# Latent attention on one core: a head's scores alternate with the last head's transposes, and a pair's products with v are issued two key tiles at a time, one step later

## The chip, the cores and the metric

One core of a Trainium2 chip. The metric is the device time of one execution in microseconds (us), lower is better. TensorE (PE in the profile, its weight loads PEld), VectorE (DVE), ScalarE (ACT) and GpSimd (POOL) each work through their own list of instructions in order and wait for each other by semaphores; SyncE (SP) issues the transfers.

## The reference

The program is a long chain: one transformer block with dilated attention, spatial gating and experts, then a retention and state-space layer with a gated feed-forward layer, then latent attention with a second feed-forward layer, all in float32. The change lies in the latent attention alone. There 512 latent tokens attend to 768 keys (256 context and 512 latent tokens), in 16 heads:

```
kv = rms_norm(ckv)                        # 768 x 256 compressed channels
k  = concat(kv @ w_uk[h], rope(k_pe))     # 64 + 32 channels, per head
q  = rms_norm(cq) @ w_uq                  # 512 x (16 x 96)
v  = kv @ w_uv                            # 768 x (16 x 64)
p  = softmax(q[h] @ k[h].T / sqrt(96))    # 512 x 768, per head
o[h] = p @ v[h]                           # 512 x 64
h1 = h + gate * (concat(o) @ w_mo)
```

## The kernel before

Everything is unrolled. The Python code records the instructions in program order; a list scheduler of the framework then fixes each engine's order once, when the program is built, with the place in the code as its priority. So the order within an engine is near that of the code, but a piece whose inputs come later may be cut up and moved behind others.

**The tiles.** Queries are cut into 4 tiles of 128 tokens (`qt`), keys into 6 tiles of 128 (`kt`), heads into 8 pairs. For each head `queries` transposes its 96 query channels (tile `qtb`, split into a high and a low part `qT`); `keys` makes a pair's keys in two pieces of 512 and 256 columns (tile `kb`, split into `kT`). `scores` makes, for each `qt`, a 128 x 768 tile `sc` by six matmuls (three split passes on 512 and on 256 columns), takes its row maximum (DVE, L1795), the exponential with its row sum (ACT, L1796), the reciprocal (DVE, L1797) and scales the probabilities `Pm` (L1798; POOL for `qt` 0, DVE for the other three). `spread(h, kt)` transposes one key tile of all four `Pm` tiles into a bank `ptb` (four transposes) and copies it out as `PTm`: DVE for `kt` 0 and 3, ACT for the other four.

**The products.** `ob` of a pair is one bank of 128 rows: the first head of the pair (`a_` = 0) writes rows 0 to 63 through the columns 0 to 63 of TensorE's array, the second (`a_` = 1) rows 64 to 127 through the columns 64 to 127. Each of the pair's 12 products (2 heads x 6 key tiles) is one float32 matmul of 512 columns, for which the trace has two records.

**The order.** A loop takes the heads one by one. Step `h` issues the keys of the next pair (every other step) and the queries of head `h` + 1, the four score tiles of head `h`, and then works on head `h` - 1: if that is the first of a pair, its six `spread`; if it is the second, `values`, in which each `spread` is followed at once by the two products of its key tile:

```
for kt in range(6):
    spread(2 * hp + 1, kt)
    for a_ in range(2):
        K.mm(ob[64 * a_:...], v[...], pts[h, kt // 2][:, kt % 2, :], kt == 0, kt == 5, ...)
```

**The buffers.** Of the eight PSUM banks `sc` has two tiles of two banks, `ptb` and `qtb` share two, `kb` and `ob` have one each. `Pm` tiles lie in the ring `wr` of 6, which also takes raw weights, so the loads of the next stage's weights `w_mo` wait until the last `Pm` tiles are read. The other stages of the program are the same before and after.

Of the kernel before, what the change touches and what calls it, by code (L numbers as in the profile page):

```python
# [7 lines left out]
F32 = mybir.dt.float32  # L8
# [21 lines left out]
# ---------------------------------------------------------------- host layout  # L30
def tile_a(w, kc=2, nb=512):
    """[K, N] -> [N/nb, K/(128 kc), 128, kc, nb], each chunk contiguous per partition."""
    k, n = w.shape
    return np.ascontiguousarray(w.reshape(k // (P * kc), kc, P, n // nb, nb).transpose(3, 0, 2, 1, 4))


def tile_b(w):
    """[K, M] -> [M/128, 128, K/128, 128]."""
    k, m = w.shape
    return np.ascontiguousarray(w.reshape(k // P, P, m // P, P).transpose(2, 1, 0, 3))  # L40


def cols(v):
    """vector [n*128] -> [128, n]."""
# [3 lines left out]
def shape_consts():  # L48
# [7 lines left out]
    c["amask"] = m[3 * P:]                                             # depends on i - j alone  # L56
    c["rinv"] = np.tile((np.float32(500000.0) ** (-np.arange(0, 16, 2, dtype=np.float32) / np.float32(16)))[None], (P, 1)).astype(np.float32)
    c["utri"] = (i[:, None] <= i[None, :]).astype(np.float32)      # [s, t]: s <= t
# [3 lines left out]
    d2 = (i[None, :] - i[:, None]).astype(np.float32)                 # [j, i]: i - j  # L62
# [14 lines left out]
def axial(n_tok, rot):  # L77
# [6 lines left out]
    cs = np.stack([np.cos(ang), np.sin(ang)]).astype(np.float32)          # [2, tok, rot/2]  # L84
# [3 lines left out]
def prep(inp):  # L88
# [3 lines left out]
    # [layer, group, column block, k chunk, 128, k (2), 512-column slab of the group, 128]  # L92
# [8 lines left out]
    cw = np.concatenate([a["ssd_conv_w_2"][0], a["ssd_conv_b_2"]], 0)        # [6, 1024]  # L101
# [28 lines left out]
    o["wspT"] = np.ascontiguousarray(a["w_spatial"][0].transpose(2, 0, 1))      # [s, g, t]  # L130
    o["bspT"] = np.ascontiguousarray(a["b_spatial"][0].T)                        # [t, g]
# [14 lines left out]
# ---------------------------------------------------------------- builder  # L146
# layer norm: columns scaled on the scalar engine and shifted on GpSimd
# [3 lines left out]
# first block: steps of the conditions on the tensor engine behind each step of its phases  # L151
# [3 lines left out]
# the first layer's conditions: thirds on the tensor engine, on the vector engine, and the latter's steps  # L155
# [3 lines left out]
class K:  # L159
    def __init__(self, tc, I, out, ctx):  # L160
# [11 lines left out]
        # token-major residual stream [128, token tile, channel]; lent to other data where the stream lies in DRAM  # L172
# [16 lines left out]
    def bcast(self, src, n, pool, name, tag=None, bufs=None, off=0):  # L189
        """DRAM row of n floats to all 128 partitions."""  # L190
# [4 lines left out]
    def spread_row(self, t, src, bank, off=0, plus=None):  # L195
        """DRAM row of 1024 floats, or the sum of two, to all 128 partitions by the tensor engine; bank(): room of 512."""
# [11 lines left out]
    def w4(self, name):  # L208
        """a [128, 1024] work tile from the raw weights' ring."""
        return self.wp.tile([P, 1024], F32, name=name, tag="wr", bufs=self.NR)  # L210

    def work(self, name):
        """a [128, 1024] work tile from all the weights' rings in turn, where few weights pass."""
# [4 lines left out]
    # raw weights chunk of at most 1024 floats per partition  # L218
# [26 lines left out]
    def mm3(self, out, A, Bm, start, stop, **kw):  # L245
        """3-pass split product; A, Bm are (h, l) pairs."""
# [4 lines left out]
    def gemm_a(self, xT, tts, kt, wsrc, chunks, ps, tag, bufs, evac, kc=2, nb=512, ahead={}):  # L251
        """token-major out = x @ W; xT(k, tt) -> (h, l) of [128, 128]; wsrc(n, c) -> DRAM. A generator."""
# [11 lines left out]
    def gemm_b(self, xT, w, kt, wsrc, ms, ps, tag, bufs, evac):  # L264
        """feature-major out^T = (x @ W)^T; xT(k) -> (h, l) views [128, w]."""
# [8 lines left out]
    def small_proj(self, xk, w, W, ps, tag, bufs, out):  # L274
        """x @ W for W [1024, 32]: partial sums in 4 column groups, added where they are transposed."""
# [8 lines left out]
    def rstd(self, ss, pool, n, scale, eps):  # L284
        """(ss*scale + eps) ** -0.5 on [128, n]."""
# [7 lines left out]
    def layernorm(self, x, g, b, pool):  # L293
        """one token tile [128, 1024] in place; g, b: [128, 1024]."""
# [14 lines left out]
    # ------------------------------------------------------------ block 1  # L309
    def block1(self, mix):  # L310
        """projections, rotary attention and spatial gating; mix: the four split halves of the mixer's output."""
# [1826 lines left out]
```

## Time and profile before

| what | us |
|---|---|
| device time, median of 3 runs (lowest to highest) | 2394.41 (2385.21 to 2395.06) |
| span of the profiled execution, first to last instruction | 2391.5 |
| latent attention, first score to last product | 1726.43 to 1962.58, 236.15 |
| one pair of heads in its middle | 28.86 |
| TensorE busy over the span | 2292.0 (96%) |

The page names no other time of the profiled execution than its span; the median lies 2.9 us above it. Times of the trace count from the first instruction. The matmuls of TensorE overlap: its next one starts before the last one's record ends, so what a piece of work costs is read from start to start, and a busy share near 100% says that the engine always had a matmul in flight, not that it ran at its best.

### The profile page before, as it was taken

To read this page: it belongs to the slowest core of one execution; us is meant where nothing else is said; L and a number is where in the kernel's file an instruction comes from. 1 tells how busy PE (TensorE), PEld (TensorE's weight loads), DVE (VectorE), ACT (ScalarE), POOL (GpSimd) and SP (SyncE) were. 2 spreads that over 40 slices of the span, in tenths; PEclk is the share of its full clock that TensorE was granted. 3 is DMA by queue.
4 is the path that set the end of the run, shared out by engine and by line. 5 is a ranking of instruction groups with operands and counts; after the bars stand their busy time and mean duration, and the time that the engine had idled before them with its cause. 6 is when DMAs were issued, how large, how long until landed. Compare 5 with 4: busy or idle time off the path is not lost.

```text
span 2391.5 us, 30148 instructions
## 1 busy us (share of the span) xinstructions
PE 2292.0 (96%) x11748; PEld 1692.9 (71%) x11748; DVE 1424.6 (60%) x2341; ACT 798.2 (33%) x1382; POOL 443.2 (19%) x331
## 2 busy tenths in 40 slices
PE   9999999999989988899999999999999999999998
PEld 7667755434467856688888888877755657888877
DVE  8766643434575587775777733575566655444446
ACT  4344333132353243432121121154355544222222
POOL 0010310233240265510000000620111114000006
PEclk9999999999989997999999999999999999999999
DMA  8655598998852011343434421123000033333231
GB/s 295 215 187 189 205 388 327 374 379 308 307 192 75 20 45 54 138 161 97 132 124 147 152 72 62 62 92 97 1 1 1 1 113 126 106 97 96 89 98 44
DMA packets 99151, 338.91 MB, mean 142 GB/s; under 512 B 14373, under 2 KB 16293, under 8 KB 99002
## 3 DMA queue, kind: packets, MB, share of 16 engines
q1 hardware_dynamic: 94394, 324.33, 38.5%
q0 software_dynamic: 4608, 12.59, 1.5%
q8 instruction: 94, 1.54, 0.3%
q14 instruction: 55, 0.45, 0.1%
HBM read 323.21 MB, written 17.86 MB: 143 GB/s over the span
## 4 chain that ended last, share of the span: by engine, by line
PE 71%; DVE 9%; issue 3%; ACT 2%; POOL 2%; DMA 1%; SPq 0%; POOLq 0%; ACTq 0%; DVEq 0%
PE gb L243 22%; PE ob L243 15%; PE ga L243 10%; PE cb L243 6%; PE gu L243 5%; PE yb L243 3%; PE sc L243 2%; PE ptb L1807 2%; DVE wl L240 1%; POOL rs_r L290 1%; PE kb L243 1%; PE ntb L920 1%; PE vb L243 1%; PE ssd_x L243 1%; PE ssd_o L243 1%
## 5 line engine op out<-in xcount | busy, mean ns | idle before, releaser
L239 ACT CAST wh<-wr 128x1024 fp32r<-128x1024 f32 (+1 forms) x239 | 249.3, 1048 | 632.0 <-PE gb L243 278.5
L240 DVE TENSOR_TENSOR wl<-wr,wh 128x1024 fp32r<-128x1024 f32 (+1 forms) x235 | 311.2, 1331 | 223.6 <-ACT wh L239 218.8
L243 PE MATMUL gb<-fh,wh 128*128 128x512 f32 x672 | 264.6, 394 | 0.0
L243 PE MATMUL gb<-fh,wl 128*128 128x512 f32 x672 | 264.2, 393 | 0.0
L243 PE MATMUL gb<-fl,wh 128*128 128x512 f32 x672 | 263.9, 393 | 0.0
L243 PE MATMUL ob<-wh,hidh 128*128 128x512 f32 x440 | 174.4, 396 | 4.8 <-DVE gob L1529 3.0
L243 PE MATMUL ob<-wl,hidh 128*128 128x512 f32 x440 | 173.0, 393 | 0.0
L243 PE MATMUL ob<-wh,hidl 128*128 128x512 f32 x440 | 173.0, 393 | 0.0
L1536 DVE TENSOR_TENSOR acc<-acc,ob 128x512 f32<-128x512 f32 x160 | 108.3, 685 | 84.5 <-PE ob L243 84.5
L860 DVE SCALAR_TENSOR_TENSOR adacc<-wr,cond,adacc 128x512 f32<-128x512 f32 x224 | 152.7, 745 | 1.5 <-DMA wr<-in_w_ada 1.5
L243 PEld LDWEIGHTS gb<-fh,wl 128*128 128x128 f32 x672 | 126.3, 188 | 28.8
L243 PEld LDWEIGHTS gb<-fl,wh 128*128 128x128 f32 x672 | 126.5, 188 | 27.9
L243 PEld LDWEIGHTS gb<-fh,wh 128*128 128x128 f32 x672 | 126.5, 188 | 27.6
L243 PE MATMUL gu<-mw,xgT 128*64 128x512 f32 x512 | 124.5, 601 | 1.3 <-issue 0.7
L243 PE MATMUL cb<-fh,wh 128*128 128x256 f32 x416 | 118.0, 284 | 0.0
L243 PE MATMUL cb<-fl,wh 128*128 128x256 f32 x416 | 117.6, 283 | 0.0
L243 PE MATMUL cb<-fh,wl 128*128 128x256 f32 x416 | 117.0, 281 | 0.0
L1538 POOL TENSOR_TENSOR acc<-acc,gate 128x1024 f32<-128x1024 f32 x10 | 28.1, 2811 | 468.7 <-DVE acc L1536 468.7
L290 POOL TENSOR_TENSOR rs_r<-rs_v,mhalf 128x1 f32<-128x1 f32 (+1 forms) x54 | 46.4, 861 | 337.2 <-DVE rs_v L288 336.9
L243 PEld LDWEIGHTS ob<-wh,hidh 128*128 128x128 f32 x440 | 83.1, 189 | 25.3 <-DVE gob L1529 3.2
L1491 DVE TENSOR_TENSOR sg<-sg,gb 128x512 f32<-128x512 f32 x42 | 28.9, 688 | 113.4 <-PE gb L243 113.3
L243 PEld LDWEIGHTS ob<-wh,hidl 128*128 128x128 f32 x440 | 83.0, 189 | 18.4
(666 smaller groups left out, 4926.4 us busy)
## 6 DMA issues: line engine op xcount, KB each, us to landing
mw<-in_w_gu SPq DMA_DIRECT2D x128, 512.0 KB, 8.1
wr<-in_w_ada SPq DMA_DIRECT2D x96, 512.0 KB, 4.3
mw<-in_w_dn SPq DMA_DIRECT2D x64, 512.0 KB, 8.8
wr<-in_w_fg SPq DMA_DIRECT2D x44, 512.0 KB, 3.6
wr<-in_w_fu SPq DMA_DIRECT2D x44, 512.0 KB, 4.3
wr<-in_w_fd SPq DMA_DIRECT2D x44, 512.0 KB, 3.7
wr<-in_w_ret SPq DMA_DIRECT2D x28, 512.0 KB, 4.0
wr<-in_w_in SPq DMA_DIRECT2D x19, 512.0 KB, 4.6
```

The source lines that it names most:

```text
L239: self.nc.scalar.copy(h, src)
L240: (eng or self.nc.vector).tensor_tensor(l, src, h.bitcast(F32), ALU.subtract)
L243: self.nc.tensor.matmul(out, lhsT, rhs, start=start, stop=stop, **kw)
L290: nc.gpsimd.tensor_tensor(r, v, self.mhalf[:, :n], ALU.pow)
L860: V.scalar_tensor_tensor(acc[:, r], W[:, k], s, acc[:, r], op0=ALU.mult, op1=ALU.add)
L920: nc.tensor.transpose(bank[:, j, i * P:i * P + P], hp[i][:, (2 * kk + j) * P:(2 * kk + j + 1) * P], self.ident)
L1491: nc.vector.tensor_tensor(t, t, out[1], ALU.mult)
L1536: V.tensor_tensor(a[:, sl], a[:, sl], ob, ALU.add)
L1538: G.tensor_tensor(a, a, gate(tt), ALU.mult)
L1807: nc.tensor.transpose(bank[:, qt * P:qt * P + P], prs[h][qt][:, kt * P:kt * P + P], K.ident)
```

## The change

`scores` now makes one tile for one `qt`, and the loop puts two `spread` of the head before behind each of the first three score tiles. `values` no longer transposes: it makes the four products of two key tiles. In a step on a pair's second head, the products of key tiles 0 and 1 stand behind the second score tile and its two `spread`, those of 2 and 3 behind the third, and those of 4 and 5 at the beginning of the next step (`late`). The loop has 18 steps for it instead of 17. The keys of the next pair are issued one step earlier, behind the queries. The counts of all matmuls, transposes, copies and transfers are the same. (The diff also takes the comments out of the file; that is left out here.)

```diff
-        def scores(h, qT):
+        def scores(h, qT, qt):
             kh, kl_ = kTs[(h // 2) % 2][h % 2]
-            prs[h] = []
-            for qt in range(NT):
-                sc = ps.tile([P, 1024], F32, name="sc", tag="sc", bufs=2)
+            sc = ps.tile([P, 1024], F32, name="sc", tag="sc", bufs=2)
...
-        def values(hp):
-            ob = pst("ob", "pv", 1)
-            for kt in range(6):
-                spread(2 * hp + 1, kt)
+        obs = {}
+
+        def values(hp, c):
+            if c == 0:
+                obs[hp] = pst("ob", "pv", 1)
+            ob = obs[hp]
+            for kt in (2 * c, 2 * c + 1):
                 for a_ in range(2):
                     h = 2 * hp + a_
                     K.mm(ob[64 * a_:64 * a_ + 64, :], v[kt // 2][:, kt % 2, h * 64:h * 64 + 64], pts[h, kt // 2][:, kt % 2, :],
                          kt == 0, kt == 5, tile_position=(0, 64 * a_))
-            V.tensor_copy(oT(hp), ob)
+            if c == 2:
+                V.tensor_copy(oT(hp), obs.pop(hp))
         qTs = self.qTs
-        for h in range(17):
-            if h < 16:
-                if h < 15:
-                    if h % 2 == 1:
-                        keys((h + 1) // 2)
-                    qTs[h + 1] = queries(h + 1)
-                scores(h, qTs.pop(h))
-            if h >= 1:
-                if (h - 1) % 2 == 0:
-                    for kt in range(6):
+        late = None
+        for h in range(18):
+            if h < 15:
+                qTs[h + 1] = queries(h + 1)
+                if h % 2 == 0 and h < 14:
+                    keys(h // 2 + 1)
+            if late is not None:
+                values(late, 2)
+                late = None
+            qT = qTs.pop(h) if h < 16 else None
+            odd = h >= 2 and h % 2 == 0
+            for i in range(NT):
+                if h < 16:
+                    scores(h, qT, i)
+                if 1 <= h <= 16 and i < 3:
+                    for kt in (2 * i, 2 * i + 1):
                         spread(h - 1, kt)
-                else:
-                    values((h - 1) // 2)
+                    if odd and i:
+                        values(h // 2 - 1, i - 1)
+            if odd and h <= 16:
+                late = h // 2 - 1
```

**Place 1: TensorE, the products of a pair in the middle of the stage.** Before, `v_13358` and `v_13359` hold key tiles 2 and 3, and 4 and 5; `Pm_14333` is the tile of the second head's first two query tiles:

```order
L243 MATMUL ob<-PTm,v_13358 64x512
L243 MATMUL ob<-PTm,v_13358 64x512 [waits Activation_49]
L1807 MATMUL ptb<-c_ident,Pm_14333 128x128 [waits PE_49]
L1807 MATMUL ptb<-c_ident,Pm_14333 128x128
L1807 MATMUL ptb<-c_ident,Pm 128x128 x2
L243 MATMUL ob<-PTm,v_13358 64x512
L243 MATMUL ob<-PTm,v_13358 64x512 [waits DVE_49]
L1807 MATMUL ptb<-c_ident,Pm_14333 128x128 [waits PE_49]
```

Now, at the same key tiles of a pair (`sc`, a score tile; `qtb`, the queries of a later head):

```order
L243 MATMUL ob<-PTm,v_13358 64x512 x4
L243 MATMUL sc<-kT_13983,qT 128x512 [waits Activation_49]
L243 MATMUL sc<-kT_13985,qT 128x512
L243 MATMUL sc<-kT_13983,qT 128x512
L243 MATMUL sc<-kT_13983,qT 128x256
L243 MATMUL sc<-kT_13985,qT 128x256
L243 MATMUL sc<-kT_13983,qT 128x256
L1755 MATMUL qtb<-c_ident,q_13545 96x128 [waits Activation_49]
L1755 MATMUL qtb<-c_ident,q_13545 96x128 x3
L243 MATMUL ob<-PTm,v_13359 64x512 x3
L243 MATMUL ob<-PTm,v_13359 64x512 [waits Activation_49]
```

The four products of two key tiles stand in a row, and a score tile and the next queries stand between two such groups. The products of key tiles 0 and 1 come as one alone and three in a row, since the scheduler has put the next pair's 256-column keys or transposes behind the first; so each pair has groups of 1, 3, 4 and 4.

**Place 2: TensorE, the step on a pair's first head.** Before, two score tiles of the head stand in a row ahead of the transposes; these are the second of them and what follows:

```order
L243 MATMUL sc<-kTh_13307,qT 128x512
L243 MATMUL sc<-kTl_13308,qT 128x512
L243 MATMUL sc<-kTh_13307,qT 128x512
L243 MATMUL sc<-kTh_13307,qT 128x256
L243 MATMUL sc<-kTl_13308,qT 128x256
L243 MATMUL sc<-kTh_13307,qT 128x256
L1807 MATMUL ptb<-c_ident,Pm 128x128 [waits PE_49,Pool_49]
L1807 MATMUL ptb<-c_ident,Pm 128x128 x2
L1807 MATMUL ptb<-c_ident,Pm 128x128 [waits DVE_49] x2
```

Now the same step goes on like this from its second score tile (all four score tiles of the step look so):

```order
L243 MATMUL sc<-kT_13987,qT 128x512 [waits Activation_49]
L243 MATMUL sc<-kT_13989,qT 128x512
L243 MATMUL sc<-kT_13987,qT 128x512
L243 MATMUL sc<-kT_13987,qT 128x256
L243 MATMUL sc<-kT_13989,qT 128x256
L243 MATMUL sc<-kT_13987,qT 128x256
L1808 MATMUL ptb<-c_ident,Pm 128x128 [waits Activation_49]
L1808 MATMUL ptb<-c_ident,Pm 128x128 x3
L1808 MATMUL ptb<-c_ident,Pm 128x128 [waits DVE_49]
L1808 MATMUL ptb<-c_ident,Pm 128x128 x3
L243 MATMUL sc<-kT_13987,qT 128x512 [waits Activation_49]
```

One score tile, eight transposes, one score tile; each score tile waits for ACT, which has to have read the tile two before it.

**Place 3: VectorE in that step.** Before (`mmx` the maxima, `mml` the reciprocals):

```order
L1795 TENSOR_REDUCE mmx<-sc 128x1 [waits PE_49]
L240 TENSOR_TENSOR qT<-qtb,qT 96x512 [waits Activation_49]
L1795 TENSOR_REDUCE mmx<-sc 128x1 [waits PE_49]
L1797 RECIPROCAL mml<-mml 128x1 [waits Activation_49]
L1808 COPY PTm<-ptb 128x512 [waits PE_49]
L1795 TENSOR_REDUCE mmx<-sc 128x1 [waits PE_49]
```

Now:

```order
L1824 COPY res<-ob 128x512 [waits PE_49]
L1796 TENSOR_REDUCE mmx<-sc 128x1 [waits PE_49]
L1809 COPY PTm<-ptb 128x512 [waits PE_49]
L1796 TENSOR_REDUCE mmx<-sc 128x1 [waits PE_49]
L1798 RECIPROCAL mml<-mml 128x1 [waits Activation_49]
L1809 COPY PTm<-ptb 128x512 [waits PE_49]
L1796 TENSOR_REDUCE mmx<-sc 128x1 [waits PE_49]
```

The pair's result is copied out ahead of the step's first maximum, and a copy of transposes stands between two maxima.

## Rows read from the trace of the kernel before

**Rows 1.** The page, part 1 (TensorE, VectorE) and the clock's line of part 2:

```profile
PE 2292.0 (96%) x11748; PEld 1692.9 (71%) x11748; DVE 1424.6 (60%) x2341; ACT 798.2 (33%) x1382; POOL 443.2 (19%) x331
PEclk9999999999989997999999999999999999999999
```

**Rows 2.** Stretches: us; PE, PEld, DVE, ACT, POOL busy (instructions); granted clock; DMA share; GB/s:

```profile
1823.37:1852.23 28.86, 28.71 (x141) 17.36 (x141) 18.10 (x33) 15.05 (x30) 4.41 (x2) 1.00 0.00 1
...
1726.43:1765.91 39.48, 36.30 (x168) 22.81 (x168) 28.55 (x67) 20.24 (x40) 9.29 (x13) 0.96 0.00 1
1938.66:1962.58 23.92, 22.44 (x97) 10.99 (x97) 15.01 (x24) 13.62 (x25) 2.59 (x1) 1.00 0.38 133
```

**Rows 3.** Chain of waits through one middle pair: start, us, what (xrecords):

```profile
1829.04 1.06 PE sc L243 x6
...
1832.26 1.00 PE ob L243 x2
...
1836.85 0.44 PE ptb L1807 x4
...
1839.47 1.01 PE ob L243 x4
...
1843.31 1.75 PE ob L243 x4
1845.06 0.59 PE ptb L1807 x4
1845.65 1.86 PE ob L243 x4
...
1848.10 1.80 PE ob L243 x4
...
1850.49 1.75 PE ob L243 x4
```

**Rows 4.** Waits in that pair: who for whom, total us, times, longest:

```profile
PEld ob L243 <- ACT PTm L1808: 1.7, 3, 0.6
...
PEld ob L243 <- DVE PTm L1808: 0.7, 1, 0.7
```

**Rows 5.** Chain of waits, the whole attention: three products in one piece:

```profile
1754.15 1.86 PE ob L243 x6
```

**Rows 6.** VectorE in that pair, groups by shape: count, busy us, mean ns:

```profile
L1795 DVE TENSOR_REDUCE mmx<-sc 128x1 f32<-128x768 f32 x8 | 7.6, 954 | 1.7 <-PE sc L243 1.4
...
L1798 DVE TENSOR_SCALAR Pm<-Pm,mml 128x768 f32<-128x768 f32 x6 | 3.7, 624 | 0.1
...
L1808 DVE COPY PTm<-ptb 128x512 f32<-128x512 f32 x4 | 2.7, 676 | 2.4 <-PE ptb L1807 2.4
```

**Rows 7.** Instructions in order of time: one score tile's softmax on VectorE and ScalarE:

```profile
1839.28 0.96 DVE L1795 TENSOR_REDUCE mmx<-sc 128x1 f32<-128x768 f32 x1 [0.38 <-PE sc L243]
...
1840.28 0.90 ACT L1796 ACTIVATE Pm<-sc,mmx 128x768 f32<-128x768 f32 x1
...
1841.30 0.16 DVE L1797 RECIPROCAL mml<-mml 128x1 f32<-128x1 f32 x1 [0.28 <-ACT Pm L1796]
```

**Rows 8.** TensorE in order of time at the beginning of the attention:

```profile
1728.37 0.61 PE L243 MATMUL sc<-kTh,qT 96*128 96x512 f32 x2 [1.22 <-DVE qT L240]
...
1730.53 0.63 PE L243 MATMUL kb<-ckTh,wk 128*128 128x512 f32 x1
1730.96 0.63 PE L243 MATMUL kb<-ckTl,wk 128*128 128x512 f32 x1
```

**Rows 9.** TensorE in order of time, end of the attention and output projection:

```profile
1944.71 1.04 PE L1807 MATMUL ptb<-c_ident,Pm 128*128 128x128 f32 x8
1945.68 1.07 PE L243 MATMUL ob<-PTm,v 128*64 128x512 f32 x2
...
1949.14 0.44 PE L1807 MATMUL ptb<-c_ident,Pm 128*128 128x128 f32 x2 [0.47 <-DVE Pm L1798]
...
1989.98 0.50 PE L243 MATMUL ga<-wl,oh 128*128 128x512 f32 x1 [1.67 <-DVE wl L240]
```

More of the change, by code (lines that the diff above doesn't have):

```diff
@@ L1777, in attention @@
         prs, pts = {}, {}
-        def scores(h, qT):
+        two = [None]
+        def scores(h, qT, qt):
             kh, kl_ = kTs[(h // 2) % 2][h % 2]
-            prs[h] = []
-            for qt in range(NT):
-                sc = ps.tile([P, 1024], F32, name="sc", tag="sc", bufs=2)
-                sl = slice(qt * P, qt * P + P)
-                for (c1, n) in ((0, 512), (512, 256)):
-                    K.mm3(sc[:, c1:c1 + n], (qT[:96, 0, sl], qT[:96, 1, sl]), (kh[:, c1:c1 + n], kl_[:, c1:c1 + n]), True, True)
-                if h % 2 and qt < 2:
-                    if qt == 0:
-                        two = big("Pm2")
-                    p_ = two[:, qt * 1024:qt * 1024 + 1024]
-                else:
-                    p_ = K.w4("Pm")
-                mx = pool.tile([P, 1], F32, name="mmx", tag="mmx", bufs=8)
-                l_ = pool.tile([P, 1], F32, name="mml", tag="mml", bufs=8)
-                V.tensor_reduce(mx, sc[:, :768], AX, ALU.max, negate=True)
-                S.activation(p_[:, :768], sc[:, :768], AF.Exp, bias=mx, accum_out=l_)
-                V.reciprocal(l_, l_)
-                (G if qt in GD else V).tensor_scalar(p_[:, :768], p_[:, :768], l_, None, op0=ALU.mult)
-                prs[h].append(p_)
+            sc = ps.tile([P, 1024], F32, name="sc", tag="sc", bufs=2)
+            sl = slice(qt * P, qt * P + P)
+            for (c1, n) in ((0, 512), (512, 256)):
+                K.mm3(sc[:, c1:c1 + n], (qT[:96, 0, sl], qT[:96, 1, sl]), (kh[:, c1:c1 + n], kl_[:, c1:c1 + n]), True, True)
+            if h % 2 and qt < 2:
+                if qt == 0:
+                    two[0] = big("Pm2")
+                p_ = two[0][:, qt * 1024:qt * 1024 + 1024]
+            else:
+                p_ = K.w4("Pm")
+            mx = pool.tile([P, 1], F32, name="mmx", tag="mmx", bufs=8)
+            l_ = pool.tile([P, 1], F32, name="mml", tag="mml", bufs=8)
+            V.tensor_reduce(mx, sc[:, :768], AX, ALU.max, negate=True)
+            S.activation(p_[:, :768], sc[:, :768], AF.Exp, bias=mx, accum_out=l_)
+            V.reciprocal(l_, l_)
+            (G if qt in GD else V).tensor_scalar(p_[:, :768], p_[:, :768], l_, None, op0=ALU.mult)
+            prs.setdefault(h, []).append(p_)
         def spread(h, kt):
@@ L1817, in values @@
                          kt == 0, kt == 5, tile_position=(0, 64 * a_))
-            V.tensor_copy(oT(hp), ob)
+            if c == 2:
+                V.tensor_copy(oT(hp), obs.pop(hp))
         qTs = self.qTs
-        for h in range(17):
-            if h < 16:
-                if h < 15:
-                    if h % 2 == 1:
-                        keys((h + 1) // 2)
-                    qTs[h + 1] = queries(h + 1)
-                scores(h, qTs.pop(h))
-            if h >= 1:
-                if (h - 1) % 2 == 0:
-                    for kt in range(6):
+        late = None
[14 more added lines that the diff above has]
+                    for kt in (2 * i, 2 * i + 1):
                         spread(h - 1, kt)
-                else:
-                    values((h - 1) // 2)
+                    if odd and i:
+                        values(h // 2 - 1, i - 1)
+            if odd and h <= 16:
+                late = h // 2 - 1
         oh, ol = ([big(f"{n}{j}", F32R) for j in range(2)] for n in ("oh", "ol"))
```

## The prediction

> **What bounds the kernel now.** I read the page's busy shares first: TensorE works 96% of the span, VectorE 60% [rows 1]. An average over three layers says little about one stage, so the stretches come next: in a middle pair TensorE has a matmul in flight for 28.71 of 28.86 us, VectorE works 18.10, ScalarE 15.05, GpSimd 4.41, the transfers nothing, and the clock is granted in full [rows 2]. The stage is bound by TensorE's own list, and what counts is what each piece of that list costs from start to start. The chain of waits shows this, and there one price stands out [rows 3]. At 1839.47 two products, four records, take 1.01 us; at 1832.26 a single product, two records, takes 1.00 (a second like it stands at 1841.72, outside the rows). So two products of the two heads, which use different halves of the array's columns, run side by side and cost what one costs. But the last four pieces, also of two products each, take 1.75, 1.86, 1.80 and 1.75. The waits say why [rows 4]: in these four pieces a product's weight load waits for its transposes' copy (`PTm`), three times for ScalarE (1.7 us in all, 0.6 each) and once for VectorE (0.7). The transposes of a key tile stand directly ahead of its two products, so the copy is not done when the second product could start, and the pair runs one after the other. All twelve products take 1.00 + 1.01 + 1.00 + 1.75 + 1.86 + 1.80 + 1.75 = 10.17 us of the 28.86.
>
> **The products, (a).** In the new order the products come in groups of 1, 3, 4 and 4, with a score tile and other work between a group and the transposes that feed it. A group of 1 costs 1.00. For a group of 3 there is a row: six records in one piece, 1.86 [rows 5]. Two of the three use the same half of the array, so that is one product's time behind another's; a group of 4 has two in each half, and side by side it should cost the same 1.86. I take 1.00 + 3 x 1.86 = 6.58 per pair. Bounds: if a group of four costs two pieces of two, 2 x 1.01 = 2.02, the pair costs 1.00 + 1.86 + 4.04 = 6.90. The last product of some groups still waits for ScalarE's copy (the first place of the order shows 3 + 1); if it lost what such a second product loses today, 1.75 - 1.01 = 0.74, once per pair, it would be 7.3. I take 6.58, since a score tile's 1.06 or more lies between the last transposes and the group, and a copy on VectorE takes 0.68 [rows 3, 6]. Saved: 10.17 - 6.58 = 3.59 per pair, times eight pairs 28.7 us; at the 6.90 price 26.2. It could be somewhat less in the first pair, where a piece of three products stands already [rows 5].
>
> **Fewer changes between transposes and products, (b).** Four transposes ahead of the late products take 0.59 from start to start, four that stand ahead of other work 0.44 [rows 3]. The 0.15 is what switching to the array's half-width products costs, or part of the product's wait. About five quartets per pair stand so: 5 x 0.15 = 0.75 at most, nothing at least, since the new groups have such borders too. With four groups left in place of some seven pieces I take 0.3 per pair, 2.4 us.
>
> **The moved score tiles and transposes, (c).** The counts are unchanged, so they cost nothing unless something is late. The order shows a new wait at the second place: each score tile waits until ScalarE has read the tile two before. What stands behind that wait on TensorE is everything: eight transposes, then the next tile. One tile to the next-but-one takes 2 x (1.06 + 8 x 0.11) = 3.9 us if nothing waits, with 0.44 / 4 = 0.11 for a transpose [rows 3]. The bank needs: 1.06 for the tile, then the maximum's start 0.2 later or so, 1840.28 - 1839.28 = 1.00 from the maximum's start to the exponential's, and 0.90 of exponential [rows 7], 3.2 in all. So there is 0.7 of slack if VectorE takes up the maximum at once. Whether it does is a question of its load. In the step on a pair's first head TensorE has four score tiles, 24 transposes, the queries' transposes and the next keys, 4 x 1.06 + 24 x 0.11 + 0.44 + 1.41 = 8.7 us (the keys' six matmuls of 512 columns are an estimate from the score tile, 1.06 us for 2304 columns). VectorE has there four maxima, four reciprocals, three scalings, two copies of transposes and the queries' split: 4 x 0.95 + 4 x 0.16 + 3 x 0.62 + 2 x 0.68 + 0.67 = 8.3 us (the split taken like a copy) [rows 6, 7]. That is 95% of TensorE's time there, and the third place of the order shows copies that wait for TensorE between the maxima, behind which the next maximum is queued. Nothing at all is the lower bound; all the slack used up and half a copy more per step is about 1 us. I take 0.2 per pair, 1.6 us. The step on the second head has the 6.58 of products besides, so TensorE takes about 16 there against some 11 of VectorE: slack. The products that move into the next step (`late`) cost nothing by being late: behind them TensorE has that step's queries and scores, and the one thing that waits for them is the copy of `ob`, 0.68 of VectorE ahead of the first maximum. If that cover were gone, it would be that 0.68 per pair. The keys of the next pair, a step earlier, go into the one of two `kTs` whose heads are through by then, and their 1.41 of TensorE only moves.
>
> **The two ends, (d).** The last pair has no scores to hide behind. The end stretch takes 23.92 us with TensorE idle for about 1.5 of it [rows 2]. By the new prices it is 23.92 - 3.9 = 20.0, of which (a) and (b) already count all, and I give another 1.1 for idles that the late group fills: 18.9. Against this a longer idle before the last group may cost clock: at 1728.37 TensorE has been idle for 1.22 us, and at 1730.53 two key matmuls of 512 columns stand 0.43 apart [rows 8] where a 512-column share of a score tile is 1.06 x 512 / 2304 = 0.24. That is the only place of the stage with a lowered clock, 0.96 over the beginning [rows 2]. I set 1.1 against it. SyncE's four loads of the `w_mo` weights stand earlier in one row; the 1.67 that the output projection waits for its weights [rows 9] could go or double. I take none of it and keep 1.7 on both sides.
>
> **Sum.** -28.7 - 2.4 + 1.6 - 1.1 + 1.1 = -29.5 against the profiled execution's span of 2391.5: 2362. The median of the three runs lies 2.9 above that span, so the forecast is **2365 us**, a pair falling from 28.86 to about 25.2 or 25.3.
>
> **The rivals.**
>
> *VectorE takes over as the bound of the step on the first head.* For it speaks the 8.3 of 8.7 above and the maxima that queue behind waiting copies; against it that VectorE has 18.10 of 28.86 now, and that 18.10 in 25.2 is still only 72% [rows 2]. If each score tile after the first two were late by 0.25 to 0.95, that gives back 0.5 to 1.9 per pair beyond the sum, 4 to 15 us; with the four-product price of 2.02 on top the time is 2369 to 2383. Still faster than before.
>
> *TensorE's clock falls in the step on the first head: slower than before.* The change gathers that step into scores and transposes alone, 24 transposes of 128 columns and no product. If the transposes did not hold up the clock, the step would run at 1.2 in place of 2.4 GHz. Fully, its 8.7 us would be 17.4: +8.7 - 3.7 = +5.0 per pair, +40, **2434 us**. It decides from about 3.7 us lost per pair, less than half the step. Against it speak the rows at the end of today's stage: from 1944.71 to 1950.8 nearly nothing but transposes stands there, eight, ten, two and three (the first and the third of these stand in the rows), with one product among them and an idle of 0.47, and eight still take 0.97 to the next start [rows 9]; the clock over the whole end stretch is 1.00 [rows 2]. The Trainium skill says in "TensorE: Matmul & The Clock Gate", Part 4: PE-mode transpose, that transposes do not count as busy work for the clock as matmuls do. By that rule this rival is what the change would bring; today's stretch of transposes at 1.00 speaks against it here, at least for 6 us, and the new step has score matmuls in between.
>
> *The change does not do what it says: the second product of a key tile is late as before.* If the copies on ScalarE stand behind exponentials, whose two score tiles now lie between transposes and products, the four pieces keep their 0.74 each, 3.0 per pair. What is left of the gain is 0.6 per pair and (b) in part: 2386 to 2395 us. Against it: a copy has a score tile and more to finish in, and ScalarE works only 15.05 of 28.86 [rows 2].
>
> **How the numbers follow.** The forecast has 0.70, the first rival 0.18, the dropped clock 0.05, no effect 0.07. About 0.5%, 12 us, is what a measurement of this kernel can tell from no change: its three runs already spread over 0.4%. Faster by more than that, below 2382, are the forecast and nearly all of the first rival: 0.87. Within it lies most of the no-effect case and the edge of the first rival: 0.08. Slower: 0.05. The forecast's own bounds: prices of 6.90 and no gain from (b) and another 1.7 at the weights give 2365 + 2.5 + 2.4 + 1.7 = 2372; with (c) at nothing, (b) in full (3.6 more) and the weights' wait gone, 2365 - 1.6 - 3.6 - 1.7 = 2358, and a run near the lower end of the spread takes 6 more, 2352. Upwards I go to 2381, which takes in most of the first rival.
>
> **What would show it.** Right: a pair's period near 25; its products as pieces of 1.00 and three of about 1.86; the weight loads' waits on `PTm` all but gone; VectorE's busy share in a pair above 70%; clock 1.00 in every middle pair; an end stretch near 19. Wrong: score tiles that wait for ScalarE's `Pm` by more than 0.5 us each (first rival); a clock below 1.00 between 1766 and 1938 (second); two-product pieces of 1.75 still there (third); or a group of four that takes 3 us or more, which would mean that four products in a row do not pair up two by two.

## The result, and the profile after

The changed kernel takes 2356.15 us (median of 4 runs, 2350.8 to 2359.68), the kernel before on the same chip 2392.3; the ratio is 0.9856, with a 95% interval of 0.9835 to 0.9877, so 29 to 39 us less. The forecast was 2365 with a range of 2352 to 2381: inside the range, the right way, 9 us too cautious.

The shares of the page hardly move, against [rows 1]; TensorE is the bound as before, busy for 39.5 us less. First the page, part 1 and the clock's line:

```profile
PE 2252.5 (96%) x11748; PEld 1688.6 (72%) x11748; DVE 1423.6 (61%) x2341; ACT 794.9 (34%) x1382; POOL 442.9 (19%) x331
PEclk9999999999989997999999999999999999999999
```

Then the stretches of the attention, as in [rows 2] (us; PE, PEld, DVE, ACT, POOL busy; granted clock; share of the transfers; GB/s): the whole from the first transposes of queries to the first matmul of the output projection; one middle pair; the beginning up to the last product of the first pair; the middle up to that of the seventh; the end:

```profile
1719.92:1925.10 205.18, 198.27 (x1110) 137.07 (x1108) 155.00 (x291) 122.26 (x248) 38.84 (x28) 0.98 0.06 19
...
1821.06:1845.44 24.38, 24.38 (x141) 17.12 (x140) 18.43 (x34) 14.52 (x31) 4.41 (x2) 1.00 0.01 2
...
1719.92:1760.57 40.65, 36.49 (x192) 26.53 (x190) 32.01 (x73) 23.75 (x48) 10.20 (x15) 0.92 0.00 1
1760.57:1903.49 142.92, 142.88 (x823) 99.48 (x821) 108.03 (x192) 84.97 (x174) 26.44 (x12) 1.00 0.00 1
1903.49:1925.10 21.61, 18.91 (x99) 11.06 (x97) 14.96 (x26) 13.54 (x27) 2.20 (x1) 0.92 0.51 175
```

Before, the whole took 237.53 (1725.05 to 1962.58), and by the same marks 40.86, 172.75 and 23.92. So by these marks the middle gives 29.8 us, the end 2.3 and the beginning 0.2. The marks do not enclose the same work, though: since the keys are issued a step earlier and the last products a step later, the beginning now has 27 matmuls of keys in place of 16 and 16 transposes of queries in place of 12. By the prices of the table below that is some 2.5 us (an estimate: 11 of 12 x 2.31, and 0.4), which moved from the middle into the beginning. Work for work, the beginning gains about 2.7 and the middle about 27.3. The attention is 32.35 shorter; behind it the program is 2.3 shorter (426.6 from the first matmul of the output projection to the end, 428.9 before): the output projection's longest wait for its weights, 1.67 in [rows 9], is 0.45 now, which is half of that. Together 34.7, which is what the ratio says, 0.0144 x 2392.3 = 34.4. The two profiled executions differ by 39.8, because this one was already 5.1 us earlier when the attention began, in a part that is the same in both; that start lay between 1714 and 1731 in the profiles of this case. In what follows the attention's own length is therefore the finer measure. It too comes from one execution of each kernel; its middle pairs repeat within 0.1 us, its two ends do not.

One middle pair in the chain of waits (start, us, what), which answers to [rows 3]:

```profile
1821.13 1.00 PE ob L243 x2
1822.13 0.92 PE kb L243 x6
1823.05 0.44 PE ptb L1808 x4
1823.49 1.86 PE ob L243 x6
1825.35 1.25 PE sc L243 x6
1826.60 0.88 PE ptb L1808 x8
1827.47 1.87 PE ob L243 x8
1829.34 1.27 PE sc L243 x6
1830.61 0.44 PE qtb L1755 x4
1831.04 1.87 PE ob L243 x8
1832.91 1.24 PE sc L243 x6
1834.15 0.88 PE ptb L1808 x8
1835.03 1.06 PE sc L243 x6
```

Eight records, four products, take 1.87, about what two took in the late pieces of before (1.75 to 1.86). All of the chain is TensorE's own work; nothing in it is a wait for another engine. The waits of that pair no longer hold a row of `ob` for a `PTm`, as [rows 4] did; what `ob` and `sc` wait for is now

```profile
PEld ob L243 <- issue: 2.4, 10, 0.3
...
PEld sc L243 <- ACT Pm L1797: 1.6, 2, 0.8
...
PEld sc L243 <- ACT kT L239: 0.8, 1, 0.8
```

Since the chain of before leaves TensorE at some places, I add up the pairs by kind from the order of time instead: each matmul from its start to the next one's start (us, in each run the fourth pair, from its first product to that of the next).

| kernel | products | transposes | scores | queries | keys | pair |
|---|---|---|---|---|---|---|
| before | 10.18 | 6.46 | 9.12 | 0.71 | 2.39 | 28.86 |
| after | 6.60 | 5.35 | 9.23 | 0.89 | 2.31 | 24.38 |
| pairs_only | 7.41 | 6.15 | 9.10 | 0.71 | 2.39 | 25.76 |
| alternate_only | 10.28 | 5.61 | 9.52 | 0.71 | 2.37 | 28.50 |
| no_delay | 7.26 | 5.21 | 9.52 | 0.71 | 2.36 | 25.06 |
| one_tile_later | 6.90 | 5.53 | 9.25 | 0.89 | 2.38 | 24.95 |
| not_late | 6.60 | 5.40 | 9.43 | 0.75 | 2.29 | 24.47 |
| one_half | 10.02 | 5.35 | 9.22 | 0.89 | 2.28 | 27.76 |
| four_together | 5.60 | 5.23 | 9.22 | 0.89 | 2.28 | 23.23 |
| together | 5.60 | 5.23 | 9.22 | 0.89 | 2.28 | 23.23 |

The products give 3.58 of the pair's 4.48 us, the transposes 1.11; scores, queries and keys together take 0.21 back.

### The profile page after: what moved, and what is told of

It reads as the page before. It is cut to its first block, busy times and chain, and to the rows that moved or that the text cites. A ratio compares the mean times of both kernels' runs of the same rounds, so it can differ in the third digit from the quotient of the medians.

```text
span 2351.7 us, 30149 instructions
## 1 busy us (share of the span) xinstructions
PE 2252.5 (96%) x11748; PEld 1688.6 (72%) x11748; DVE 1423.6 (61%) x2341; ACT 794.9 (34%) x1382; POOL 442.9 (19%) x331
## 4 chain that ended last, share of the span: by engine, by line
PE 72%; DVE 8%; issue 3%; POOL 2%; ACT 2%; DMA 0%; POOLq 0%; SPq 0%; DVEq 0%; ACTq 0%
PE gb L243 22%; PE ob L243 14%; PE ga L243 10%; PE cb L243 6%; PE gu L243 5%; PE sc L243 3%; PE yb L243 3%; PE ptb L1808 2%; DVE wl L240 1%; POOL rs_r L290 1%; PE kb L243 1%; PE vb L243 1%; PE ntb L920 1%; PE ssd_x L243 1%; PE tpm L687 1%
```

## The experiments

The theory: a pair's products get cheap because products of the two heads, in two halves of the array's columns, run side by side as soon as no copy is awaited; fewer borders between transposes and products and fewer waits of the transposes give the rest. The rivals: it is the alternation of scores and transposes that pays; or it is only that TensorE no longer waits, and the halves have nothing to do with it; or the two heads' products must be neighbours in the list for it; or the step later is the necessary part. The runs, with the attention's length in the profiled execution (205.18 after, 237.53 before). The ratio is to the kernel before on the same chip; by it alone only alternate_only and one_half stand clear of the change (0.9835 to 0.9877), so the readings rest on the attention's length and on the pair:

| run | attention, us | median, us | ratio to before (95%) |
|---|---|---|---|
| pairs_only | 212.19 | 2370.16 | 0.9908 (0.9873 to 0.9943) |
| alternate_only | 236.97 | 2381.20 | 0.9969 (0.9952 to 0.9986) |
| no_delay | 212.70 | 2358.53 | 0.9879 (0.9845 to 0.9913) |
| one_tile_later | 210.74 | 2363.54 | 0.9890 (0.9858 to 0.9923) |
| not_late | 205.31 | 2353.05 | 0.9859 (0.9828 to 0.9890) |
| same_half | 205.24 | 2356.12 | 0.9867 (0.9831 to 0.9904) |
| one_half | 232.12 | 2383.84 | 0.9969 (0.9947 to 0.9990) |
| four_together | 199.08 | 2350.49 | 0.9849 (0.9819 to 0.9879) |
| keys_late_first | 204.86 | 2357.34 | 0.9873 (0.9849 to 0.9897) |
| splits_gpsimd | 204.93 | 2351.46 | 0.9848 (0.9824 to 0.9873) |
| together | 197.52 | 2346.95 | 0.9829 (0.9804 to 0.9853) |

**pairs_only**, the kernel before with the products of two key tiles together and nothing else:

```diff
             for kt in range(6):
-                spread(2 * hp + 1, kt)
+                if kt % 2 == 0:
+                    spread(2 * hp + 1, kt)
+                    spread(2 * hp + 1, kt + 1)
                 for a_ in range(2):
```

> The kernel before with one part of the change: the products of two key tiles together, behind the eight transposes of those two tiles; scores, keys and steps stand as before and nothing is issued a step later. Theory (the gain is products of the two heads running side by side once no copy is awaited, and fewer borders between transposes and products): most of the gain is there without the alternation, since the first two products of a group of four hide the copy that the other two need. A pair's products cost 7.0 to 7.6 us (10.17 before, 6.60 after), a pair's period is 25.3 to 26.2, the time 2365 to 2374. Rival (it is the alternation of scores and transposes that pays, the products gain by the way): products still near 10, a period of 28 or more, 2385 or more.

The theory's side, in every number: products 7.41, a period of 25.76. The chain of waits shows the last eight of a pair's products, each four directly behind their transposes:

```profile
1836.53 1.02 PE ptb L1807 x8
1837.56 2.17 PE ob L243 x8
1839.73 1.03 PE ptb L1807 x8
1840.75 2.22 PE ob L243 x8
```

Four products with a late copy cost 2.2 where two with a late copy cost 1.75 to 1.86, as it should be if the first two products cover most of the wait of the others. This part alone gives 25.3 of the 32.35 us of the attention.

**alternate_only**, the changed kernel with each key tile's products behind its own transposes again (`values` makes one key tile):

```diff
                     for kt in (2 * i, 2 * i + 1):
                         spread(h - 1, kt)
-                    if odd and i:
-                        values(h // 2 - 1, i - 1)
-            if odd and h <= 16:
-                late = h // 2 - 1
+                        if odd:
+                            values(h // 2 - 1, kt)
```

> The changed kernel with the products of each key tile again directly behind its own transposes, in the same step; scores still alternate with transposes, keys still stand a step earlier. Theory: the second product of a key tile waits for its copy as before, so a pair's products cost 9.5 to 10.5 us and the period is 27.5 to 28.9; time 2383 to 2394, within 0.4% of the kernel before. Rival (the alternation pays): a period of 24.4 to 26 and a time below 2372.

The pair takes 28.50, its products 10.28, and the pieces of 1.75 to 1.85 are back, each a quartet of transposes apart:

```profile
1836.40 1.80 PE ob L243 x4
1838.20 0.59 PE ptb L1808 x4
1838.79 1.75 PE ob L243 x4
```

So the alternation by itself is not the gain: the attention is 0.6 us shorter. The whole program came out a little below the expected 2383, and in its profile 4.5 us of that lie behind the attention, where the output projection waits for no weights at all. What the alternation does give is 0.85 of the transposes, of which the more broken-up scores take 0.40 back.

**no_delay**, the alternation and the pairs without the step later: in the same place `if odd: values(h // 2 - 1, i)` behind the two `spread`, and no `late`.

> The changed kernel without the step later: scores alternate with transposes, products come two key tiles at a time, but directly behind the eight transposes of their own two key tiles. Theory: two of the four products hide most of the other two's copy, as in the kernel with the pairs alone (2.17 to 2.22 for a group of four there); with groups of 1, 3, 4 and 4 the products cost 1.00 + 1.86 + 2.2 + 2.2 = 7.3, transposes 5.3 to 5.7, scores 9.3 to 9.5: a period of 25.0 to 25.6, a stage 5 to 9 us longer than the changed kernel's 205.2. Rival (the step later is what matters, behind a waiting product everything is late): a period above 26.2.

A period of 25.06 and products of 7.26, groups of four at 2.17 and 2.22 again. The attention is 7.5 longer than after, which is what the step later is worth. In a middle pair it is 0.68, of which the products are 0.66; the scores, more cut up here, take 0.29 more, the transposes and queries 0.32 less. The rest lies nearer the two ends. In the program's time the step later does not show clear of the noise (2358.53 against 2356.15).

**one_tile_later**, the step later, but one key tile at a time:

```diff
-                    if odd and i:
-                        values(h // 2 - 1, i - 1)
+                        if odd and i:
+                            values(h // 2 - 1, kt - 2)
```

> The changed kernel with the products one step later, but one key tile at a time: two products, four transposes, two products, four transposes. Theory: what counts is that the copy is done, so two products still cost 1.01; with the scheduler's groups of 1, 1, 2, 2, 2 and 4 the products cost 6.9 us, and two or three more borders from transposes to products cost 0.19 each (a quartet ahead of products takes 0.59 in the changed kernel, half of eight ahead of a score tile 0.40). Period 24.9 to 25.4, time 2359 to 2365. Rival (two key tiles at a time are needed to hide something else): two products cost 1.75 or more and the period is above 27.

Its chain of waits:

```profile
1802.37 1.01 PE ob L243 x4
1803.38 1.24 PE sc L243 x6
1804.62 0.44 PE ptb L1808 x4
1805.06 1.01 PE ob L243 x4
1806.07 0.59 PE ptb L1808 x4
1806.66 1.01 PE ob L243 x4
```

Two products cost 1.01 whenever their copy is old, 6.90 per pair in all as expected; two key tiles at a time are not needed for that. The added borders cost less than I had set, 0.18 of transposes per pair in all. With no_delay this makes lateness and size two ways to the same end: the copy is covered by other work or by other products.

**same_half** was to put two products of the same half next to each other, by exchanging the two inner loops of `values`.

> The changed kernel with the four products of a group in another order: both key tiles of the first head, then both of the second, so that two products that use the same half of the array's columns stand next to each other. Theory (two heads run side by side only as neighbours in the list): a group of four costs three single slots in place of two, 2.7 to 2.8 us for 1.87, in two groups of a pair; the group of one and three stays. Period 26.0 to 26.3, time 2369 to 2373. Rival (the only thing that counts is that no product waits for a copy): 24.4 and 2356, no change to the changed kernel.

A middle pair takes 24.37, its groups 1.87 to 1.88, the attention 205.24: the rival's numbers. And the order did change. TensorE's list of the program built from this kernel has first head, first head, second head, second head in every middle group of four, where the changed kernel alternates. The trace agrees. These are its groups of four in a middle pair:

```profile
1822.64 1.87 PE ob L243 x8
...
1826.21 1.88 PE ob L243 x8
```

In either kernel's list the third and the fourth product of a pair's last group signal their end. After, in one middle pair, the second records of both start at 1807.92, when the group ends. In this run that of the third product starts at 1802.25, 0.02 behind the second record of the first product, and that of the fourth at 1803.11. So the third product, the first of the other half, ran beside the first and ahead of the second. The theory of neighbours fails: the two heads run side by side though they do not alternate, so TensorE does not keep to the order of its list between the two halves here; what the text ahead says of the engines' order is too strict for this case. The rival's reason, that the halves play no part, is what the next run tests. (In the first and the last two pairs the scheduler cut the groups in another way, so the whole attention's 205.24 is no exact repeat.)

**one_half** takes the second half away from five of the six key tiles:

```diff
-                    K.mm(ob[64 * a_:64 * a_ + 64, :], v[...], ...,
-                         kt == 0, kt == 5, tile_position=(0, 64 * a_))
+                    r_ = 64 * a_ if kt == 5 else 0
+                    K.mm(ob[r_:r_ + 64, :], v[...], ...,
+                         kt == 5 if r_ else kt + a_ == 0, kt == 5, tile_position=(0, r_))
```

> The changed kernel, but the second head's products of key tiles 0 to 4 also use the first 64 columns of the array and add onto the first head's rows, so that only the products of key tile 5 stand in two halves; counts, order and waits are those of the changed kernel. The sums of the attention are other ones by that. Theory (a group is cheap because products in different halves run side by side): each further product in one half costs 1.86 - 1.00 = 0.86, so groups of 1, 3, 4 and 4 cost 1.00, 2.72, 3.58 and 2.72, together 10.0 us for 6.60; a pair's period is 27.8, the stage about 27 us longer than after, time 2380 to 2387. Rival (it is only that no product waits for a copy any more): products 6.6, period 24.4, 2356.

The groups of 1, 3, 4 and 4 in its chain of waits:

```profile
1842.15 1.00 PE ob L243 x2
...
1844.47 2.72 PE ob L243 x6
...
1849.31 3.58 PE ob L243 x8
...
1854.59 2.72 PE ob L243 x8
```

The expected prices, 10.02 in all and a period of 27.76, with the same order, and no row of the pair's waits has `ob` waiting for a `PTm`. Running side by side is nearly the whole of the products' gain: without it, 26.9 of the attention's 32.35 us are gone again. A product's half of the columns and the rows of the bank that it writes go together here, so the runs do not tell which of the two must differ. The Trainium skill's "TensorEngine Tiling (Array Packing)", in Tiling Modes, Key Properties, says that tiles work independently, loads and matmuls of different ones in parallel; these rows agree, with 2.72 and 3.58 for what takes 1.87 in two halves.

**four_together** lets the second head's product be recorded first (`for a_ in (1, 0)`), which keeps the scheduler from sending the pair's first product, ready long before, ahead by itself.

> The changed kernel with the second head's product of a key tile recorded ahead of the first head's; the scheduler then leaves the first product of a pair with the other three, and the groups are 4, 4 and 4. Theory: 3 x 1.87 = 5.6 us of products for 6.60, and a border less from transposes to products, 0.19: a period of 23.2 to 23.4 for 24.4, a stage some 8 to 9 us shorter than after, time 2345 to 2351. Rival (VectorE, at 18.4 of 24.4 now, is what sets the first head's step): 24.2 or more, no gain beyond 2 us.

Groups of 4, 4 and 4 at 1.87, products 5.60, a period of 23.23, all as expected; VectorE does not hold it. But the attention is only 6.1 shorter in place of 8 to 9: between the first score matmuls of the fourth and of the last head it is 137.63 for 142.92, 5.3 less over six pairs. Four of them gain the 1.15, the first and the last of the six 0.4 and 0.3, and what lies outside gains 0.8. That this is faster than the changed kernel rests on the attention's length; the intervals of the two ratios overlap.

**not_late**, the last four products at the end of their own step (`values(h // 2 - 1, 2)` in place of `late = ...`).

> The changed kernel with the last four products of a pair at the end of their own step, behind its last score tile, and not at the beginning of the next behind the queries' transposes. Theory (a score tile between the last transposes and the products is enough for the copies): products 6.6, period 24.2 to 24.6, stage within 2 us of 205.2. Rival (the copies on ScalarE stand behind exponentials and come later than a score tile): 0.7 more per pair, a period of 25 or more.

24.47 a pair, products 6.60, the attention 205.31: the same. A score tile of 1.25 between the last transposes and the products covers the copies.

**keys_late_first**, the second pair's keys in the second step:

```diff
+                if h == 1:
+                    keys(1)
                 qTs[h + 1] = queries(h + 1)
-                if h % 2 == 0 and h < 14:
+                if h % 2 == 0 and 0 < h < 14:
                     keys(h // 2 + 1)
```

> The changed kernel with one of its parts undone at one place: the keys of the second pair stand at the beginning of the second step, as before, and not in the first step; all later keys stay a step earlier. Theory: the idle of 3.49 us at 1729.11, in which TensorE waits for the one bank of keys, and a part of the stretch at half clock behind it go, and the first products of the stage come 3 to 5 us earlier after the stage's start (24.4 us after, 23.4 before); the middle pairs stay at 24.4. Rival (another wait of the beginning takes its place, VectorE's maxima and splits being late anyway): less than 1.5 us.

Here the rival is right, narrowly. After, TensorE waits 3.49 us at the beginning for the bank of keys, and then runs at half clock:

```profile
1729.11 0.55 PE L243 MATMUL kb<-ckTh,wk 128*128 128x256 f32 x1 [3.49 <-DVE kT L240]
```

```profile
1729.11:1735.44 6.33, 6.33 (x22) 5.56 (x22) 3.71 (x7) 4.37 (x10) 2.21 (x1) 0.50 0.01 3
```

In this run both are gone, the clock is granted in full from 1716 to 1757, and other idles stand in their place (TensorE in order of time):

```profile
1725.13 0.50 PE L243 MATMUL sc<-kTh,qT 96*128 96x512 f32 x1 [1.73 <-ACT Pm L1797]
...
1728.75 0.50 PE L243 MATMUL sc<-kTh,qT 96*128 96x512 f32 x1 [0.67 <-ACT Pm L1797]
...
1733.21 1.22 PE L1808 MATMUL ptb<-c_ident,Pm 128*128 128x128 f32 x8 [0.72 <-ACT PTm L1809]
```

VectorE works for 11.88 of 13.00 us there, and what TensorE waits for comes from ScalarE:

```profile
1722.00:1735.00 13.00, 9.75 (x59) 7.70 (x58) 11.88 (x25) 7.96 (x18) 2.21 (x1) 1.00 0.01 1
```

The stage's first product comes at 26.3 us, later and not earlier than after's 24.4. By the last product of the second pair the run is 1.3 us ahead, and 1.4 at the last head's first score, counted from the start of the attention. Over the whole attention only 0.3 is left, since its end takes 22.67 in place of 21.61, at a clock granted at 0.85 in place of 0.92. So the idle of 3.49 and the 6.33 at half clock cost 1.4 us together where they stood, about a fifth of what they look like (an estimate: the idle, and half of the 6.33), because the first heads' softmax on VectorE and ScalarE holds TensorE there in any case.

**splits_gpsimd**, the output's splits of pairs 0 to 6 on GpSimd (`K.split(oT(k), ..., G if k < 7 else None)`).

> The changed kernel with the splits of the finished pairs 0 to 6 (ol, on VectorE between the last maxima, copies and scalings) moved to GpSimd. Theory: at the end VectorE sets the pace, three splits of 0.6 to 0.95 stand between the last maxima and scalings, so the idles of 1.13, 0.89 and 0.68 ahead of the last transposes shrink, and the stretch at half clock with them: the end, from the last pair's first product to the output projection, goes from 14.2 to 11 to 12.5 us. Rival (ScalarE's copies or the clock's dip from other idles keep it): 13.5 or more.

13.1 us from the last pair's first product to the output projection: between the two answers. The idles at the end are 0.81, 1.11 and 0.68 in place of 1.13, 0.89 and 0.68, and the clock dips again. With the splits away the waits are for the last scalings themselves; as a gain this is open, 0.25 us of the attention, and the time's interval overlaps that of the change.

**together**, the last three edits that could pay, in one kernel.

> The three edits together: products in groups of 4, 4 and 4, the second pair's keys in the second step, the splits of pairs 0 to 6 on GpSimd. Theory: the gain of the first is in the middle, that of the others at the ends, so they add up: middle pairs at 23.2, a stage of 196.5 to 198.5 us (199.1 with the groups alone), time 2345 to 2350. Rival (an idle that goes at an end comes back as another, and the clock dips anyway): 199 or more, no difference to the groups alone.

Middle pairs at 23.23, the attention 197.52, the time 2346.95: as expected, 7.7 us less attention than after and 1.6 less than with the groups alone. By the time alone the intervals of the ratios still overlap with the change's. The end is still there, 22.26 us from the last head's first score at a clock granted at 0.85 (TensorE, from the last transposes):

```profile
1904.94 3.38 PE L243 MATMUL ob<-PTm,v 128*64 128x512 f32 x8
1908.25 1.09 PE L1808 MATMUL ptb<-c_ident,Pm 128*128 128x128 f32 x8
1909.27 3.65 PE L243 MATMUL ob<-PTm,v 128*64 128x512 f32 x16
```

The first four products take 3.3 with the clock granted at 0.56, the next eight 3.6 at 1.00.

## Why the prediction was right, and where it was off

**The bound.** Right: TensorE's own list sets the time before and after; a middle pair is busy for 24.38 of 24.38.

**(a), the products.** Right to the number: 6.60 for the forecast 6.58, 3.58 saved for 3.59. That a group of four costs what three cost was read off one row [rows 5], and one_half shows the reason for it. That the other half's product must stand next to it was no part of the prediction, and same_half shows that it need not. The 3 + 1 of the order, in which the last product has a wait of its own on ScalarE, cost nothing: the copy is done by then, as not_late shows with even less time between.

**(b), the transposes.** Mis-sized: 0.3 per pair taken, with 0.75 as the most, 1.11 measured, outside its own bound. Two things were in it. The borders I had counted are real: eight transposes ahead of products take 0.97 from start to start, eight ahead of a score tile 0.80.

```profile
1826.43 1.04 PE L1808 MATMUL ptb<-c_ident,Pm 128*128 128x128 f32 x8
1827.40 1.94 PE L243 MATMUL ob<-PTm,v 128*64 128x512 f32 x8
...
1833.99 1.04 PE L1808 MATMUL ptb<-c_ident,Pm 128*128 128x128 f32 x8
1834.79 0.48 PE L243 MATMUL sc<-kTh,qT 96*128 96x512 f32 x1
```

But the step on the first head held waits of its own before: eight transposes ahead of the keys took 1.19 there, and a row of the waits of that pair, which I had not put to account, says that transposes waited 0.8 us for ScalarE's copies:

```profile
1826.89 1.04 PE L1807 MATMUL ptb<-c_ident,Pm 128*128 128x128 f32 x8
1828.08 0.39 PE L243 MATMUL kb<-ckTh,wh 128*128 128x256 f32 x1
```

```profile
PEld ptb L1807 <- ACT PTm L1808: 0.8, 1, 0.8
```

alternate_only separates the two: with the products as bad as before, the transposes still fall from 6.46 to 5.61. So most of the 1.11 comes from the alternation, not from fewer borders (pairs_only: 0.31).

**(c), the moved scores.** Right in sum, largely by luck: 0.2 per pair forecast, scores, queries and keys together 0.21. But 0.18 of it are the queries' transposes, of which four now stand ahead of products (1830.44 to 1830.97, 0.53 for 0.36 before), a border as in (b) and not a late VectorE. The new wait of the score tiles for ScalarE shows in the weight loads, 0.8 us at the longest, and TensorE has a matmul in flight all the while. VectorE's share of a pair is 18.43 / 24.38 = 76%, and even 18.59 of 23.23 in four_together sets nothing: the first rival did not come.

**(d), the ends.** Too large. The forecast took 3.69 us (3.59 + 0.3 - 0.2) from each of the eight pairs, and 18.9 us for the end, or 20.0 with 1.1 for the clock. Measured, work for work, the beginning gains about 2.7 and the end, at 21.6, 2.3. At the beginning the softmax of the first heads holds TensorE up (keys_late_first); at the end TensorE waits three times for the last scalings and a copy, 2.7 us in all, and the group behind them runs at a lowered clock:

```profile
1917.28:1920.49 3.21, 3.21 (x7) 0.76 (x6) 0.69 (x1) 0.00 (x0) 0.00 (x0) 0.57 1.00 389
```

The prediction allowed 1.1 us for that; three products in 3.21 where 1.86 is the price at full clock are 1.35 of it. Its real error was to count a full pair's gain in the first and the last pair, where TensorE also waits for other engines. The six middle pairs were forecast at 22.1 us and gave about 27.3, the surplus mostly from (b); the two ends were forecast at 7.4 and gave about 5.0. The errors partly cancel: 29.5 forecast for the attention, 32.35 measured. What lies behind the attention, on which I had not bet, gave 2.3 more; over the profiles of this case that part takes between 424.4 and 429.7 us, so the 2.3 is not shown to belong to the change. The four weight loads in one row are not shown to be its cause: pairs_only has them in the same row, and its output projection waits 2.37 and 1.26 for weights.

**The clock.** The rival on the other side fell clearly. The step of four score tiles and 24 transposes stands in the middle stretch, 142.92 us with the clock granted at 1.00, 2.4 GHz. The Trainium skill, in "TensorE: Matmul & The Clock Gate", Part 4: PE-mode transpose, says that the full clock does not engage for transposes; by that the clock would suffer there. In this mixture of transposes and score matmuls it does not, and the measurement decides. The clock fell only behind idles, at the two ends.

**No effect.** The third rival, that the second product stays late, describes alternate_only, not the change.

## What to carry to other kernels

When two matmuls can share the array, compare what a pair of them costs when both are ready with what it costs when one waits: the difference, here 0.8 of 1.8 us, is bought by any work put between a copy and its reader, and as well by other ready matmuls put ahead of the late one. Take such a gain in full only from the repeats in which that engine is the bound; the first and the last, where the chain fills and drains, gave about half of it here. And compare stretches by the work that they hold: a mark set at the same product enclosed 2.5 us more work after the change than before. A scheduler that fills gaps can pull a ready product out of its group: one recorded order exchanged for the other was worth 1.0 us of products per pair.

## What the runs showed of the hardware that was not expected

Products that keep to one half of the array cost 1.00 for the first and 0.86 for each that follows, and two in different halves 1.01 together: from these prices the products of a pair come out within 0.02 us in all six kernels of the table in which none waits for a copy (after, one_tile_later, not_late, one_half, four_together, together). In same_half, where the list has two products of one half and then two of the other, four cost 1.87 as well: the third starts beside the first, ahead of the second.

Half clock does not always cost what it seems to: 6.33 us of TensorE at 0.50 at the beginning of the attention, taken away together with the 3.49 us of idle ahead of it, were worth 1.4 us. At the end, idles of 1.13, 0.89 and 0.68 with short transposes between them were followed by 0.57 for 3.2 us, and behind that the clock is at 1.00 again. In same_half the first of these three idles is missing, the clock stays at 1.00, and the same end takes 19.97 in place of 21.61:

```profile
1899.68:1919.65 19.97, 18.27 (x98) 10.80 (x97) 15.00 (x26) 13.56 (x28) 2.21 (x1) 1.00 0.49 178
```
